# Operand splits behind accumulator hand-backs, earlier weight loads and a copy in two parts, in a hybrid attention and recurrence block

## The chip, the cores and the metric

The kernel runs as one program on one core of a Trainium2 chip. The core has a matrix engine (TensorE, "PE" in the profile, with its weight loads as "PEld"), a vector engine (VectorE, "DVE"), a scalar engine (ScalarE, "ACT"), GpSimd ("POOL"), SyncE ("SP", which here does nothing but issue transfers), and DMA engines that move data between HBM and the on-chip memory. TensorE's results go to PSUM, eight banks of 128 x 512 fp32; everything else that is on chip lies in SBUF.

The metric is the time of one execution on the device, in microseconds (us), lower being better. Times are medians of several executions.

## The reference

One encoder block over a sequence of 1024 tokens with 1024 channels, all in fp32. `@` is a matrix product.

```python
xn = rmsnorm(x, norm1_g)
q_sb, k_sb, v_sb, f_raw, i_hg, q_hg, g_hg, gate_sb, gate_hg = split(xn @ w_in)
# stick-breaking attention, 8 heads of 64, strictly causal (s < t)
z = q @ k.T / sqrt(64)
A[t, s] = sigmoid(z[t, s]) * prod_{s<j<t} (1 - sigmoid(z[t, j]))
o_sb = A @ v
# HGRN2 recurrence, 4 heads of 128, in chunks of 64 tokens
f = lb + (1 - lb) * sigmoid(f_raw)
S_t = diag(f_t) S_{t-1} + (1 - f_t) i_t^T ;  o_t = S_t^T silu(q_t)
o_hg = rmsnorm(o_hg) * silu(g_hg)
# merge by gates, output projection, MLP, final norm
merged = sigmoid(gate_sb + b) * (o_sb @ w_o_sb) + sigmoid(gate_hg + b) * (o_hg @ w_o_hg)
h = x + merged @ w_out
h = h + square(relu(rmsnorm(h, norm2_g) @ w_ff1)) @ w_ff2
return rmsnorm(h, final_g)
```

## The kernel before

**Products.** An fp32 matrix is kept as two parts of the reduced type `fp32r`, a high part (a cast of the value) and a low part (the value less its high part). `hi_lo` makes both: the cast is a copy on ACT (L144), the subtraction runs on DVE (L149) and waits for the cast. This is called a split below. A product of two split matrices is three matmuls for each step of the contraction (high by high, high by low, low by high), so a `128 x 512` result with 512 channels in the contraction takes twelve matmuls, issued by `three` at L121. The large products use Strassen-like forms: sums and differences of blocks stand as operands, and there are fewer products than blocks.

**Order of the work.** The Tile framework schedules the program: it keeps data dependences, gives each engine a queue that runs in order, and otherwise follows the order of the program. `after(ins, earlier)` adds an order on an engine without any wait in hardware. TensorE's work is in two lanes ("main" and "fill", L88 to L117), each in order. `load` (L129) issues a transfer from SP and ties each to the one before it, so that these leave SP in the order of the program; a load whose buffer is not yet free holds up every load behind it. In the output stage, `in_turn` (L136) also ties ACT's and DVE's instructions to the order of the program, among them all casts and subtractions of `hi_lo`.

**Buffers.** SBUF holds 40 slots of 128 x 1024 fp32 (`slot`), 10 halves of 128 x 512 (`half`), and the pool `wts` with two buffers for each of three tags: `raw` (weights as loaded), `whi` and `wlo` (their two parts). A new tile of a tag waits until the tile two before it has been read for the last time. `Unit` (L419) is a set of weights: `load` puts its pieces in `raw` buffers, or in slots for those pieces that its tuple `roomy` names; `split` loads what is not loaded, and makes the high and low parts (in slots where the unit is `wide`).

**Stages that the change touches**, in order of time:

- Attention. For each head and each block of 128 queries, `scores` makes the products with the keys, ACT takes two sigmoids into `bt` and `rm`, and `weights` (L768) runs a scan over the keys on DVE (L778), multiplies (`mul`, L157), and copies the result `bt` by a transfer from SP into `wr`, an `fp32r` tile. `turn` (L818) transposes `wr` on TensorE in parts of four key blocks, which ACT copies out of PSUM (`pw`), and `values` multiplies by the values (`po`). The last query block, number 7, has 1024 keys; its scan and product are made in two parts, columns 512 to 1022 first, then 0 to 511, and one copy of all 1024 columns follows. Its `turn` transposes columns 512 to 1023 first, then calls `between`, the value products of the head before, and then transposes columns 0 to 511.
- Gate products of the first kind. `raw_job(cb)`, for eight column blocks, loads and splits the weights `wga*` and makes three products. `st.prefetch()` inside splits the next job's weights and loads those of the job after it.
- Attention output. `sb_job(cp)`, four jobs, multiplies the attention output by `w_o_sb` (`wo00` to `wo03`, 512 KB each). Its unit is loaded by the prefetch, into `raw` buffers.
- Gate pairs. `gates` goes through eight `GatePair` objects. Each starts product 6 into bank `gX` (`x6`), whose result DVE adds into `gu` (L1201), then product 5 into bank `gY` (`y5`), then product 7 on top of `gX` (`x7`), a product with the HGRN2 output, and product 3 on top of `gY`. Between `y5` and `x7` the next pair's weights are split (`n.split`): two subtractions on raw weights (`wg*r`), a split of four blocks, one more subtraction and a second split. The casts and low parts are tied behind the DVE addition `gu` by `behind`; the first two subtractions are not.
- Output projection. `out_start` makes the Strassen forms of `merged @ w_out`. Each form has a weight operand (`wout*`, for the forms named `11`, `21`, `2`, `3`, `4`, `1` and `22`) and a merged operand (`m2`, `m3`, `ma`, `m1`, `m4`, two tiles each, read back from the scratch tensors `fd`). A form runs over four token blocks of twelve matmuls each. Forms `11` and `12` accumulate in four banks `pwW`, forms `2`, `3` and `a` in four banks `pwX`; after each token block DVE adds or subtracts the bank into the residual tiles `h` (L1204 for the subtractions), and with that it hands the bank back to TensorE, which starts the next form on the same bank. `out_operands` loads and splits the operands of a form two forms ahead, with its splits at the place where it is called. `out_block_done` makes forms `1` and `4` with banks `pwY`.
- First weights of the MLP. `UpPair.load`, `split` and `sums` bring the first `w_ff1` pairs and make sums of blocks of them in place, on DVE, four subtractions for each pair. The sums of the first two pairs stand in the fourth loop of `out_start`; the loop over `out_block_done` follows (L2228), then the MLP.

## Time and profile before

| | |
|---|---|
| median of 3 runs | 1426.67 us (1425.78 to 1429.88) |
| the profiled execution's own time | 1428.57 us |
| its span, first to last instruction | 1426.8 us |
| mean granted TensorE clock | 0.996 |
| ACT busy | 677.1 us (47%) |
| DMA, mean over the span | 172 GB/s |

The stretches that hold the stages named above, in a view of busy time by windows (length, then busy time and number of instructions of PE, PEld, DVE, ACT and POOL, then the granted clock, the share of the DMA engines' time that is busy, and GB/s):

```profile
0.00:120.00 120.00, 115.41 (x738) 101.55 (x740) 84.60 (x123) 80.81 (x172) 26.05 (x71) 1.00 0.58 166
120.00:500.00 380.00, 379.13 (x3677) 325.52 (x3674) 235.15 (x350) 188.16 (x444) 43.26 (x106) 1.00 0.41 110
500.00:590.00 90.00, 89.97 (x729) 74.80 (x728) 70.14 (x99) 42.50 (x87) 18.86 (x25) 1.00 0.71 209
590.00:725.00 135.00, 132.09 (x581) 108.63 (x580) 104.08 (x151) 44.77 (x61) 10.79 (x20) 1.00 0.55 181
725.00:800.00 75.00, 72.10 (x318) 59.11 (x317) 54.61 (x65) 36.69 (x48) 11.11 (x19) 0.98 0.73 231
800.00:1426.80 626.80, 619.61 (x2772) 513.34 (x2770) 448.16 (x536) 284.19 (x387) 30.01 (x43) 1.00 0.55 196
```

Attention and the recurrence take the first 500 us; the gate products of the first kind and the attention output end near 590, the gate pairs near 725, the output projection soon after 800, and the MLP takes the rest.

How to read the lines of the profile below. A line of a group or of one instruction has its start (for one instruction), its length or the group's busy time in us, the engine, the line of the code, the operation, then `out<-in` by the names of the tiles, the sizes as partitions x elements, and in square brackets the idle time just before it with what ended that wait. `SPq` is SyncE's queue, where a line is the issue of a transfer; a line with `DMA` is the flight of one, from its start to its landing. A line such as `PE gX L121 <- DVE gu L1201: 2.9, 2, 2.4` belongs to the list of waits: TensorE's work for tile `gX` waited for DVE's work on `gu`, 2.9 us in all, in two waits, the longest 2.4. In the list of stretches, "granted clock" is TensorE's clock as a share of full speed.

### The profile page before, as it was taken

The page shows a single profiled execution, that of the slowest core. Times are in us where ns is not written, and L with a number is a line of the kernel's source. Part 1 is how long each engine was busy: PE and PEld are TensorE (multiplying, and loading weights), DVE is VectorE, ACT ScalarE, POOL GpSimd, SP SyncE. Part 2 cuts the span into 40 slices and gives each one's busy share as a digit, 9 for nine tenths or more (in the row PEclk, how much of TensorE's full clock was granted, in tenths as well). Part 3 has the DMA queues.
Part 4 walks back from the last instruction along what each step waited for, and adds up shares of the span by engine and source line. Part 5 has one row for each costly group of instructions (what it writes and reads, how often), then busy time and mean ns, then how long its engine had stood idle before and what let it go on. Part 6 is the DMA issues. An engine that isn't in the chain of part 4 may idle for free.

```text
span 1426.8 us, 22645 instructions
## 1 busy us (share of the span) xinstructions
PE 1408.3 (99%) x8806; PEld 1182.9 (83%) x8806; DVE 996.7 (70%) x1320; ACT 677.1 (47%) x1197; POOL 140.1 (10%) x283
## 2 busy tenths in 40 slices
PE   9999999999999999999999999999999999999998
PEld 8888888988888888788887888888888888888886
DVE  6587677656635586788659897766666658668765
ACT  7576666643323354332244764454444443524343
POOL 3121121110000022000010300000000000000042
PEclk9999999999999999999999999999999999999999
DMA  7356366632203458744587515443346974776825
GB/s 215 97 169 185 104 170 150 154 79 81 74 24 111 112 173 242 235 156 159 182 243 249 181 39 186 162 151 135 140 157 235 342 268 155 273 276 235 285 95 182
DMA packets 167139, 244.78 MB, mean 172 GB/s; under 512 B 26700, under 2 KB 97912, under 8 KB 167032
## 3 DMA queue, kind: packets, MB, share of 16 engines
q1 hardware_dynamic: 151192, 200.07, 41.3%
q0 software_dynamic: 11520, 34.61, 9.9%
q10 hardware_dynamic: 4320, 8.65, 1.7%
q8 instruction: 69, 1.13, 0.3%
q14 instruction: 38, 0.31, 0.1%
HBM read 162.55 MB, written 61.87 MB: 157 GB/s over the span
## 4 chain that ended last, share of the span: by engine, by line
PE 85%; DMA 4%; DVE 2%; ACT 1%; issue 0%; POOL 0%; SPq 0%; DVEq 0%; POOLq 0%
PE pm L121 21%; PE pX L121 9%; PE pW L121 6%; PE pY L121 6%; PE pji L121 3%; PE pga L121 3%; PE pjf L121 3%; PE pjg L121 3%; PE pjq L121 3%; PE gX L121 3%; PE pyh L121 3%; PE gY L121 3%; PE pys L121 2%; PE po L121 2%; PE z L121 2%; PE pjqk L121 2%
## 5 line engine op out<-in xcount | busy, mean ns | idle before, releaser
L778 DVE TENSOR_TENSOR_SCAN rm<-rm,bits 128x511 f32<-128x511 f32 (+7 forms) x72 | 87.3, 1222 | 39.7 <-ACT rm L756 39.6
L144 ACT CAST whid<-w 128x1024 fp32r<-128x1024 f32 x30 | 31.6, 1053 | 154.6 <-PE pm L121 90.3
L121 PE MATMUL pm<-wlod,sh 128*128 128x512 f32 x240 | 93.5, 389 | 0.0
L121 PE MATMUL pm<-whid,sh 128*128 128x512 f32 x240 | 93.4, 389 | 0.0
L121 PE MATMUL pm<-whid,sl 128*128 128x512 f32 x240 | 93.4, 389 | 0.0
L121 PE MATMUL pm<-tl,sh 128*128 128x512 f32 (+1 forms) x210 | 81.3, 387 | 0.0
L121 PE MATMUL pm<-th,sl 128*128 128x512 f32 (+1 forms) x210 | 81.3, 387 | 0.0
L121 PE MATMUL pm<-th,sh 128*128 128x512 f32 (+1 forms) x210 | 81.3, 387 | 0.0
L149 DVE TENSOR_TENSOR wlod<-w,whid 128x1024 fp32r<-128x1024 f32 x30 | 36.7, 1222 | 59.2 <-ACT whid L144 59.2
L149 DVE TENSOR_TENSOR sl<-sa,sh 128x1024 fp32r<-128x1024 f32 x56 | 68.2, 1217 | 0.5 <-ACT sh L144 0.5
L144 ACT COPY wT<-pw 128x128 f32<-128x128 f32 (+3 forms) x96 | 43.9, 483 | 34.8 <-PE pw L818 29.9
L144 ACT CAST sh<-sa 128x1024 fp32r<-128x1024 f32 x56 | 57.2, 1046 | 6.0 <-DMA sa<-ad 6.0
L1955 POOL TENSOR_SCALAR fss<-fss 128x1 f32<-128x1 f32 x8 | 4.5, 562 | 562.1 <-ACT fsc L1950 561.6
L157 DVE TENSOR_TENSOR bt<-bt,rm 128x511 f32<-128x511 f32 (+7 forms) x72 | 48.9, 687 | 8.8 <-ACT bt L759 3.0
L121 PEld LDWEIGHTS pm<-wlod,sh 128*128 128x128 f32 x240 | 45.1, 188 | 9.9 <-DVE wlod L149 0.4
L121 PEld LDWEIGHTS pm<-whid,sh 128*128 128x128 f32 x240 | 45.0, 188 | 9.4
L121 PEld LDWEIGHTS pm<-whid,sl 128*128 128x128 f32 x240 | 45.0, 188 | 9.2
L756 ACT ACTIVATE rm<-z 128x511 f32<-128x511 f32 (+4 forms) x96 | 48.3, 505 | 4.4 <-DMA wr<-bt 2.3
L759 ACT ACTIVATE bt<-z 128x512 f32<-128x512 f32 (+3 forms) x96 | 48.6, 508 | 3.4 <-DMA wr<-bt 2.5
L121 PE MATMUL pX<-sql,t1h 128*128 128x512 f32 x128 | 50.0, 391 | 0.1
L121 PE MATMUL pX<-sqh,t1l 128*128 128x512 f32 x128 | 49.8, 389 | 0.0
L121 PE MATMUL pX<-sqh,t1h 128*128 128x512 f32 x128 | 49.8, 389 | 0.0
(913 smaller groups left out, 4334.6 us busy)
## 6 DMA issues: line engine op xcount, KB each, us to landing
w<-in_w_ff_dram SPq DMA_DIRECT2D x72, 512.0 KB, 5.0
sa<-ad SPq DMA_DIRECT2D x56, 512.0 KB, 6.8
ad<-a SPq DMA_DIRECT2D x32, 256.0 KB, 4.3
ad<-s SPq DMA_DIRECT2D x16, 512.0 KB, 5.4
tw<-in_w_out_dram POOLq DMA_DIRECT2D x24, 256.0 KB, 4.5
x<-in_x_dram SPq DMA_DIRECT2D x8, 512.0 KB, 8.5
wr<-bt SPq DMA_DIRECT2D x8, 512.0 KB, 3.1
xnl<-xnh POOLq DMA_DIRECT2D x8, 512.0 KB, 13.8
```

What stands on the lines that cost most here:

```text
L121: return pe(nc.tensor.matmul(*a, **k))
L144: hi_last[0] = after(in_turn("act", nc.scalar.copy(dst, src)), hi_behind[0])
L149: nc.vector.tensor_tensor(out=dst, in0=src, in1=hi.bitcast(F32), op=ALU.subtract),
L157: return nc.vector.tensor_tensor(out=out, in0=a, in1=b, op=ALU.mult)
L756: nc.scalar.activation(rm[:, s0 + c0 - 1 : s0 + m - 1], z[:, c0:m], AF.Sigmoid, scale=-0.125)
L759: nc.scalar.activation(bt[:, s0 : s0 + e], z[:, :e], AF.Sigmoid, scale=0.125)
L778: nc.vector.tensor_tensor_scan(out=rr, data0=rr, data1=bits[:, 1024 - nk + a : 1024 - nk + b][:, ::-1], initial=rm[:, b : b + 1] if i else ...
L1955: nc.gpsimd.tensor_scalar(out=ssq, in0=ssq, scalar1=1.0 / D, scalar2=EPS, op0=ALU.mult, op1=ALU.add)
```

## The change

The diff does the following.

- In `weights` the copy into `wr` moves into the loop over the two parts, so that each part is copied right after its product; the copy of the first part of query block 7 takes columns 512 to 1023 (with the last column, which GpSimd sets to zero). Blocks with one part still have one copy.
- In `raw_job`, in the seventh and eighth jobs, two `w_o_sb` units each are loaded right after the prefetch, and piece 0 of these units lies in a slot in place of a `raw` buffer. Before, the prefetch asked for one of them in each of these two jobs and for the others during the attention output.
- In `GatePair.split` the first subtraction is tied behind `gu` too.
- `out_operands` now takes one weight operand or one merged operand, loads it, and returns its split, which the caller runs later; the tiles for the high and low parts of a merged operand are taken at the split. The weight units `3` and `1` lie in slots, the others in `raw` buffers. In the loops of `out_start` each load comes as early as before or earlier, and each split stands behind the hand-back of a token block.
- The weight sums of the first two MLP pairs move from the last loop of `out_start` into the loop over `out_block_done`, behind the hand-backs of blocks 0 and 1, and the splits of those pairs move behind the hand-backs of their loop.

```diff
--- before.py
+++ after.py
@@ -773,6 +773,7 @@
         bt, rm = zs[h, qb]
         cut = qb == NT - 1
         parts = ((512, nk - 1), (0, 512)) if cut else ((0, nk - 1),)
+        wr = slot_n(f"wr{h}_{qb}", nk, F32R)
         for i, (a, b) in enumerate(parts):
             rr = rm[:, a:b][:, ::-1]
             nc.vector.tensor_tensor_scan(
@@ -784,8 +785,8 @@
                 op1=ALU.max,
             )
             weighted[0] = mul(bt[:, a:b], bt[:, a:b], rm[:, a:b])
-        wr = slot_n(f"wr{h}_{qb}", nk, F32R)
-        nc.sync.dma_start(wr[:, 0:nk].bitcast(F32), bt[:, 0:nk])
+            cs = slice(a, nk if i == 0 else b)
+            nc.sync.dma_start(wr[:, cs].bitcast(F32), bt[:, cs])
         zs[h, qb] = wr
 
     def turn(h, qb, between):
@@ -1297,6 +1298,9 @@
                 u.split_t()
             st.prefetch()
             hi_behind[0] = None
+            if cb >= KT - 2:
+                for unit in sb_units[2 * (cb - KT + 2) : 2 * (cb - KT + 3)]:
+                    unit.load()
             yield from steps_of(p4, 1, 0, 1, 4, True)
             add(p14, p1, p4)
             if cb == 3 or cb == KT - 1:
@@ -1367,9 +1371,13 @@
         yield from range(4)
         gp[0].split()
 
+    sb_units = []
+
     def sb_job(cp):
         src = W_OSB[:, cp * 256 : (cp + 1) * 256].rearrange("(k p) c -> p k c", p=P)
         unit = Unit(f"wo0{cp}", [[(0, 256, src)]])
+        unit.roomy = (0,)
+        sb_units.append(unit)
 
         def body():
             if cp == 0:
@@ -1439,7 +1447,7 @@
             cb = self.cb
             r0, r1 = self.raw
             s0, s1 = slice(0, 512), slice(512, 1024)
-            sub(r0[:, s0], r0[:, s1], r0[:, s0])
+            after(sub(r0[:, s0], r0[:, s1], r0[:, s0]), behind)
             sub(r1[:, s0], r1[:, s1], r0[:, s0])
             h, l = (
                 wpool.tile([P, 1024], F32R, tag=t, name=f"{t}g{cb}") for t in ("whi", "wlo")
@@ -1601,28 +1609,29 @@
     out_form = {"11": out_unit("11", out_block(0, 0))}
     merged = {}
 
-    def out_operands(w=(), m=(), behind=False):
-
-        for n in w:
-            out_form[n] = out_unit(n, tw[int(n)] if len(n) == 1 else out_block(int(n[0]) - 1, int(n[1]) - 1))
-            out_form[n].split()
-        for n in m:
-            merged[n] = []
-            raw = []
-            for kp in range(2):
-                r = slot(f"m{n}r{kp}")
-                load(r.rearrange("p (k t) -> p k t", k=2), fd[n][kp])
-                h, l = slot(f"m{n}h{kp}", F32R), slot(f"m{n}l{kp}", F32R)
-                merged[n].append((h, l))
-                raw.append(r)
-
-            def split(n=n, raw=raw):
-                for (h, l), r in zip(merged[n], raw):
-                    hi_lo(h, l, r)
-
-            if behind:
-                return split
-            split()
+    def out_operands(w=None, m=None):
+
+        if w:
+            unit = out_form[w] = out_unit(
+                w, tw[int(w)] if len(w) == 1 else out_block(int(w[0]) - 1, int(w[1]) - 1)
+            )
+            unit.roomy = (0, 1) if w in ("3", "1") else ()
+            unit.load()
+            return unit.split
+        merged[m] = []
+        raw = []
+        for kp in range(2):
+            r = slot(f"m{m}r{kp}")
+            load(r.rearrange("p (k t) -> p k t", k=2), fd[m][kp])
+            raw.append(r)
+
+        def split():
+            for kp, r in enumerate(raw):
+                h, l = slot(f"m{m}h{kp}", F32R), slot(f"m{m}l{kp}", F32R)
+                merged[m].append((h, l))
+                hi_lo(h, l, r)
+
+        return split
 
     def out_product(ps, a, w, tb, start):
         open_block("fill")
@@ -1652,7 +1661,8 @@
             nc.scalar.dma_start(hres[4 + tb], X[rows(4 + tb), :])
         for tb in range(4):
             if tb == 0:
-                out_operands(["21"])
+                out_operands("21")()
+                w2 = out_operands("2")
             oW[tb] = bank(f"pwW{tb}")
             out_product(oW[tb], "11", "11", tb, True)
             for ins in (
@@ -1662,19 +1672,20 @@
                 in_turn("act", ins)
             h = hres[4 + tb][:, right]
             turn_dve(sub(h, h, oW[tb]))
-            if tb == 0:
-                out_operands(["2"])
             if tb == 1:
-                m2 = out_operands(m=["2"], behind=True)
+                m2 = out_operands(m="2")
+                w2()
         m2()
         for tb in range(4):
+            if tb == 0:
+                w3 = out_operands("3")
+            if tb == 1:
+                m3 = out_operands(m="3")
             out_product(oW[tb], "12", "21", tb, False)
             h = hres[4 + tb][:, left]
             turn_dve(add(h, h, oW[tb]))
-            if tb == 0:
-                out_operands(["3"])
-            if tb == 1:
-                out_operands(m=["3"])
+            if tb == 2:
+                w3()
         for tb in range(4):
             oX[tb] = bank(f"pwX{tb}")
             out_product(oX[tb], "2", "2", tb, True)
@@ -1682,30 +1693,42 @@
             turn_dve(sub(h, h, oX[tb]))
             nc.gpsimd.dma_start(hres[tb], X[rows(tb), :], accum_op=ALU.add)
             if tb == 0:
-                out_operands(["4"])
+                m3()
+                w4 = out_operands("4")
             if tb == 1:
-                out_operands(m=["a"])
+                ma = out_operands(m="a")
+            if tb == 3:
+                w4()
         for tb in range(4):
             out_product(oX[tb], "3", "3", tb, False)
             h = hres[tb][:, right]
             turn_dve(sub(h, h, oX[tb]))
             if tb == 0:
-                out_operands(["1"])
+                ma()
+                w1 = out_operands("1")
             if tb == 1:
-                out_operands(m=["1"])
+                m1 = out_operands(m="1")
             if tb > 1:
                 pairs[tb - 2].load()
+            if tb == 3:
+                w1()
 
         for tb in range(4):
             u = pairs[tb % 2]
-            (u.split if tb < 2 else u.sums)()
             out_product(oX[tb], "a", "4", tb, False)
             h = hres[tb][:, left]
             turn_dve(add(h, h, oX[tb]))
+            if tb == 0:
+                m1()
+                w22 = out_operands("22")
+            if tb == 1:
+                m4 = out_operands(m="4")
+            if tb < 2:
+                u.split()
             if tb == 2:
-                out_operands(["22"])
+                w22()
             if tb == 3:
-                out_operands(m=["4"])
+                m4()
 
     def out_block_done(tb):
 
@@ -2227,6 +2250,8 @@
 
     for tb in range(NT):
         out_block_done(tb)
+        if tb < 2:
+            first[tb].sums()
         norm_from(tb)
         if tb > 0:
             norm_to(tb - 1)
```

## The prediction

> **What bounds the kernel now.** First the page, then the list of what TensorE waited for, then busy time and clock in the stretches around its longest waits.
>
> ```profile
> span 1426.8 us, 22645 instructions
> PE 1408.3 (99%) x8806; PEld 1182.9 (83%) x8806; DVE 996.7 (70%) x1320; ACT 677.1 (47%) x1197; POOL 140.1 (10%) x283
> PE pw L818 <- DMA wr<-bt: 2.9, 3, 1.8
> PE gX L121 <- DVE gu L1201: 2.9, 2, 2.4
> PE pwX L121 <- DVE h L1204: 2.9, 2, 2.1
> 115.59:119.00 3.41, 1.65 (x12) 1.05 (x10) 2.69 (x3) 3.37 (x9) 1.08 (x3) 1.00 0.89 249
> 119.00:122.41 3.41, 3.41 (x20) 2.25 (x21) 3.28 (x6) 1.75 (x3) 0.52 (x1) 0.50 0.57 185
> 590.04:593.45 3.41, 2.17 (x10) 1.47 (x8) 1.96 (x4) 0.00 (x0) 0.37 (x1) 1.00 1.00 343
> 593.45:596.86 3.41, 2.22 (x10) 1.84 (x11) 1.46 (x3) 2.84 (x4) 0.17 (x1) 1.00 0.67 268
> 757.30:760.71 3.41, 1.35 (x7) 1.06 (x7) 3.16 (x4) 2.68 (x4) 0.00 (x0) 1.00 0.55 180
> 760.71:764.12 3.41, 3.41 (x10) 2.67 (x9) 3.41 (x5) 1.40 (x2) 0.00 (x0) 0.50 0.97 307
> ```
>
> TensorE is busy 1408.3 of 1426.8 us. The change removes none of its matmuls, so all it can win is idle time (18.5 us) and time at a lowered clock. The list shows three waits of 2.9 us each that belong to the places the diff touches. In the window rows the columns are the stretch, its length, busy time of PE, PEld, DVE, ACT, POOL, then granted clock, DMA share and GB/s. Where TensorE was busy 1.65 or 1.35 us of a 3.41 us stretch, the stretch after it was granted 0.50; where 2.43 us of waiting straddled two stretches (busy 2.17 and 2.22), the clock stayed at 1.00. So two of the three waits cost a second time: 3.41 us at half clock lose 3.41 x 0.5 = 1.71 us of work each.
>
> **Part A, the longest copy in two.** For query block 7 the weights are made in two column parts, and one copy of 1024 columns waits for both.
>
> ```profile
> 110.32 0.69 DVE L157 TENSOR_TENSOR bt<-bt,rm 128x511 f32<-128x511 f32 x1 [0.19 <-issue]
> 113.24 5.16 DMA wr<-bt
> 118.53 0.50 PE L818 MATMUL pw<-ident_r,wr 128*128 128x128 f32 x4 [1.76 <-DMA wr<-bt]
> 58.86 0.51 PE L818 MATMUL pw<-ident_r,wr 128*128 128x128 f32 x4 [0.30 <-DMA wr<-bt]
> 209.33 0.34 PE L818 MATMUL pw<-ident_r,wr 128*128 128x128 f32 x2 [0.87 <-DMA wr<-bt]
> 202.08 7.11 DMA wr<-bt
> 155.47 4.05 PE po L121 x40
> ```
>
> The first four transposes of this block read columns 512 to 1023, exactly the part that DVE had multiplied by 111.01 (110.32 + 0.69). The copy started at 113.24, after the second part, and landed 5.16 us later. Split, the first half can start at about 111.1, 2.1 us sooner. With as long a flight it lands at 116.3; TensorE wants it at 118.53 - 1.76 = 116.8. The second half still lands near 118.4, but is read only after the value products between (40 instructions, 4.05 us at full clock), about 121. So 1.76 goes, with its slow window (1.71), and the 0.30 at 58.86 as well. The wait at 209.33 is for a block with one copy, 7.11 us on its way, and stays. Added: eight DMA issues on SP, below 0.5 us each, while SP stands idle most of the time; queued behind them are weight loads, which would wait for the mul, at most 2 us. I cost them at nothing, and at 0.87 (the worst wait left here) if loads bunch. The gain is the earlier start; what the smaller size saves in flight I leave out. **A: 1.76 + 0.30 + 1.71 = 3.77 us.**
>
> **Part B, gate splits behind hand-backs.**
>
> ```profile
> 591.49 0.69 DVE L1204 TENSOR_TENSOR wg4r<-wg4r 128x512 f32<-128x512 f32 x1 [3.43 <-DMA wg4r<-in_w_in_dram]
> 593.90 0.68 DVE L1201 TENSOR_TENSOR gu<-pr,gX 128x512 f32<-128x512 f32 x1
> 594.64 0.50 PE L121 MATMUL gX<-gsh,tgh 128*128 128x512 f32 x1 [2.43 <-DVE gu L1201]
> 694.40 0.68 DVE L1201 TENSOR_TENSOR pr<-pr,gY 128x512 f32<-128x512 f32 x1
> 698.18 0.39 PE L121 MATMUL gY<-gsh,whig 128*128 128x512 f32 x1
> 600.37 2.77 PE gY L121 x12
> ```
>
> `gu` reads the bank that TensorE wants back. DVE is in order, and the next pair's first subtraction stood ahead of `gu`, waiting 3.43 us for its weights. Tied behind `gu`, it lets `gu` run when product 6 ends, one product of twelve matmuls (2.7 us) before TensorE asks at 592.2: 2.43 us gone. What waits now is the split: three subtractions (0.69 + 1.28, two of them in the second row) move from before `gu` to after it, in each of seven pairs. Their products are a whole pair later, so TensorE does not see them; the nearest reader behind them on DVE is `pr<-pr,gY`, which frees a bank 698.18 - 695.08 = 3.1 us before it is wanted. Moved subtractions (1.97) plus one exposed ACT cast (1.05, as for `wout3h` below) make 3.0: just covered, and DVE may take `gY` first. Bounds: 0 to 7 pairs x 0.5 us; I take 0, by that row. The other wait on `gu` (2.9 - 2.4 = 0.5) comes in the last pair, which has no next one to split: it stays. The attention-output weights now come in slots, so the two raw buffers of the gate weights fall free sooner; that makes `wg4r` early and helps B a second time, at no gain of its own. **B: 2.43 us.**
>
> **Part C, output-projection splits behind hand-backs.**
>
> ```profile
> 747.24 1.05 ACT L144 CAST wout3h<-wout3r 128x1024 fp32r<-128x1024 f32 x1 [0.90 <-DMA wout3r<-tw]
> 749.75 1.05 ACT L144 CAST m3h<-m3r 128x1024 fp32r<-128x1024 f32 x1 [0.16 <-DMA m3r<-fd]
> 740.24 1.22 DVE L149 TENSOR_TENSOR m2l<-m2r,m2h 128x1024 fp32r<-128x1024 f32 x1 [5.10 <-ACT m2h L144]
> 748.33 1.22 DVE L149 TENSOR_TENSOR wout3l<-wout3r,wout3h 128x1024 fp32r<-128x1024 f32 x1 [0.72 <-ACT wout3h L144]
> 750.07 2.35 DVE L149 TENSOR_TENSOR m3l<-m3r,m3h 128x1024 fp32r<-128x1024 f32 x2
> 753.53 0.68 DVE L1204 TENSOR_TENSOR h<-h,pwX 128x512 f32<-128x512 f32 x1
> 758.69 0.68 DVE L1204 TENSOR_TENSOR h<-h,pwX 128x512 f32<-128x512 f32 x1
> 754.36 0.47 PE L121 MATMUL pwX<-wout3h,m3h 128*128 128x512 f32 x1 [0.84 <-DVE h L1204]
> 759.43 0.50 PE L121 MATMUL pwX<-wout3h,m3h 128*128 128x512 f32 x1 [2.06 <-DVE h L1204]
> 731.69 1.96 SPq L129 DMA_DIRECT2D m3r<-fd  x2
> 747.63 2.32 SPq L129 DMA_DIRECT2D wout4r<-tw  x2
> ```
>
> Both waits are hand-backs (`h<-h,pwX`) queued on DVE behind splits of late weights; the second stood behind `wout4`, whose load left SP only at 747.63. I lay DVE out in the new order from these rows. `wout3` lands as before; its split ends at 749.5. Then the fourth add of form 12 (0.6), the first hand-back of form 2 (to 750.7), `m3` (2 x 1.2, cast done at 750.8, to 753.1), and three hand-backs (to 754.9). TensorE ends form 2 at 754.36 - 0.84 = 753.5 and needs bank 0 (750.7) and both `m3` tiles (the second after six matmuls, 754.9): no wait; block 1, at 756.2, has its bank since 753.7. `wout4r` is no longer held to 747.63 by the raw buffers, since `wout3r` is in slots: it can be issued behind `m3r`, about 734, and lands in order behind it, near 753; its split ends near 757, needed at 764. The later sets (`ma`, `1`, `m1`, `22`, `m4`) lie the same way, with 4 us or more. So 0.84 + 2.06 goes, and the window at half clock. If the splits slip by more than the 0.4 us between `m3` and form 3, part of it stays: bounds 0 to 4.6, value 4.6 by the rows. **C: 2.90 + 1.71 = 4.61 us.**
>
> **Part D, loads asked sooner, and weight sums.**
>
> ```profile
> 514.47 1.57 SPq L129 DMA_DIRECT2D wga7r<-in_w_in_dram  x2
> 523.39 1.22 DVE L1204 TENSOR_TENSOR wga7r<-wga7r,wga7r 128x1024 f32<-128x1024 f32 x1 [4.45 <-DMA wga7r<-in_w_in_dram]
> 533.66 0.37 SPq L129 DMA_DIRECT2D wo02r<-in_w_o_sb_dram  x1
> 550.57 1.05 ACT L144 CAST wo02h<-wo02r 128x1024 fp32r<-128x1024 f32 x1 [7.22 <-DMA wo02r<-in_w_o_sb_dram]
> 788.62 1.28 DVE L1589 SCALAR_TENSOR_TENSOR hn<-h,n_y,g2b 128x1024 f32<-128x1024 f32 x1 [1.61 <-POOL n_y L243]
> ```
>
> Asked near 517, the 2 MB of attention-output weights miss the crowd in which `wo02r` took 17 us. TensorE lost nothing there, so nothing is won. Cost: they follow `wga7r`, on which DVE waits 4.45 us; in order behind it they take nothing, sharing with it up to 9 us (17 less the 7.6 from 515.7 to 523.3). I take 0: the transfers above landed in the order asked. The eight sums (0.69 each by the `wg4r` row, 5.5 us) leave a full DVE for one that stands idle 1.61 us before `hn`; the first hand-back there comes sooner by more. 0.
>
> **Sum.** The profiled execution took 1428.57 us, 1.77 beside its span. 1428.57 - (3.77 + 2.43 + 4.61) = 1428.57 - 10.81 = **1417.8 us**. The median of the runs shown, 1426.67, is 1.9 lower; their spread, 1425.78 to 1429.88, is what one or two slow windows make. A run without stalls has none to lose, so I keep 1417.8; if the 1.9 belongs to the profiling, it is 1415.9.
>
> [...]
>
> **Rivals.**
> 1. Operands late. Form 3 finds `m3` instead of the bank: the 0.4 us of C is too thin, and its waits and dip return as operand waits. 1417.8 + 4.6 = 1422.4. For it: `wout3r` took 16 us. Against: bank and operands come 0.4 us early or more by the rows.
> 2. The first half of the copy flies longer beside new traffic: A is lost, 1421.6. For: one copy took 7.11 us before 209.33. Against: 5.16 suffices.
> 3. The dips come from something other than these waits and stay: 1421.2. Against: both follow them at once.
> 4. The change does not do what it says: the order on the engines comes out as before, or equal waits take the place of the old ones: 1428.6.
> 5. Slower: in the output stage eight transfers of 512 KB (`wout4`, `ma`, `wout1`, `m1`) now stand beside `m2`, `wout3` and `m3`. At 307 GB/s they take 13.7 us. If the queue shares its rate instead of finishing in order, `m3` lands up to that much later: 11 us of waiting, 1.7 of slow clock, and some 4 more for `m2`, whose split ends at 741.46, 1.2 us before its use (four blocks of 2.7 before 753.5): 1417.8 + 16.7 = 1434.5. It decides from a delay of 13 us in all. Against it: the casts of `wout3` and `m3` were released one after another, 1.2 to 2 us apart, which is order.
>
> **How the numbers follow.** Forecast 0.60 (1415.5 to 1420), rivals 0.12, 0.06, 0.05, 0.08, 0.09. A measurement of this kernel tells 0.3% (4.3 us) from nothing: faster is below 1422.4. Forecast, 2, 3 and half of 1 give 0.77; half of 1 and rival 4 give 0.14; rival 5 gives 0.09. From 1414.5 (1415.9 less the waits that I leave in) to 1423.5 some 0.83 lie.
>
> **What would show it.** The list of TensorE's waits without `wr<-bt` at the first two places, without `gu` near 590 and without `h` near 755; `gu` ahead of `wg4r` on DVE; `wout4r` issued before 740; a granted clock of 1.00 from 20 to 1400 us. Wrong: a wait of `pwX` on `m3` or `wout3`, of `gY` on `pr`, of `pga` on `wga7wlo` above 0.5, or a window at 0.50 with none of these before it.

## The result, and the profile after

The changed kernel took 1417.88 us (median of 6 runs, 1416.70 to 1418.38), the kernel before 1427.09 us (6 runs, 1422.42 to 1432.32): a ratio of 0.9931, with a 95% interval of 0.9909 to 0.9953. The forecast was 1417.8. The total was right; two of the three terms that made it were too large, and the loads, which were costed at nothing, were worth more when put in alone than either of these two was when undone. The experiments below show this.

The page of the kernel after, its first lines:

```profile
span 1415.9 us, 22663 instructions
PE 1403.9 (99%) x8806; PEld 1180.7 (83%) x8806; DVE 997.4 (70%) x1320; ACT 678.3 (48%) x1197; POOL 143.4 (10%) x283
```

The list of what TensorE waited for, in the kernel after (total, times, longest):

```profile
PE warm L121 <- POOL ident masks.py:199: 2.2, 1, 2.2
PE hnt L124 <- DVE hn L1597: 1.0, 1, 1.0
PE pX L121 <- DVE a L1202: 0.6, 1, 0.6
PE pX L121 <- DVE sql L149: 0.3, 1, 0.3
PE pjqk L121 <- DVE xnl L325: 0.3, 1, 0.3
```

The span of the profiled execution is 10.9 us shorter, with the same 8806 matmuls. TensorE's idle time fell from 18.5 to 12.0 us, and its busy time by 4.4 us, of which two slow stretches (2 x 1.71) make 3.4. None of the three groups of 2.9 us is left, nor the smaller waits in them that the forecast had left in (0.87 at 209 us, 0.5 in the last gate pair). A wait of `hnt` for `hn`, 1.0 us, is new.

Busy time and clock in the stretches that answer to those before (PE, PEld, DVE, ACT, POOL, then granted clock, DMA share, GB/s):

```profile
114.84:118.26 3.42, 3.42 (x28) 2.60 (x28) 2.50 (x2) 3.33 (x8) 0.50 (x2) 1.00 1.11 286
...
745.83:749.25 3.42, 3.42 (x17) 2.83 (x16) 3.42 (x4) 2.83 (x3) 0.00 (x0) 1.00 1.04 389
```

Form 3 began at 744.88 here, 9.5 us sooner than before, so the second row lies sooner too. TensorE is full and the clock is whole at both places. The timeline of the kernel after, around the first gate pair and in the output projection (start, length, engine, instruction):

```profile
584.60 0.69 DVE L1202 TENSOR_TENSOR gu<-pr,gX 128x512 f32<-128x512 f32 x1 [3.38 <-PE gX L121]
585.21 0.68 DVE L1205 TENSOR_TENSOR wg4r<-wg4r 128x512 f32<-128x512 f32 x1
...
725.89 2.05 SPq L129 DMA_DIRECT2D wout4r<-tw  x2
...
734.00 0.39 PE L121 MATMUL pwX<-wout2h,m2h 128*128 128x512 f32 x1
...
735.56 2.14 ACT L144 CAST wout3h<-wout3r 128x1024 fp32r<-128x1024 f32 x2 [5.01 <-DMA wout3r<-tw]
737.99 1.05 ACT L144 CAST m3h<-m3r 128x1024 fp32r<-128x1024 f32 x1 [0.29 <-DMA m3r<-fd]
739.28 1.05 ACT L144 CAST m3h<-m3r 128x1024 fp32r<-128x1024 f32 x1 [0.24 <-DMA m3r<-fd]
```

The order is the one forecast: `gu` runs when product 6 ends and the weights' subtraction follows it; `wout4r` is asked for at 725.89, before 740; and the operands of form 3 land one after another, about 1.3 us apart, though `wout4` had been asked for behind them. So the slower rival, in which these transfers share their rate, did not come about.

### The profile page after: what moved, and what is told of

Same layout as the page of the kernel before. It is cut to its first block, busy times and chain, and to the rows that moved or that the text cites. A ratio compares the mean times of both kernels' runs of the same rounds, so it can differ in the third digit from the quotient of the medians.

```text
span 1415.9 us, 22663 instructions
## 1 busy us (share of the span) xinstructions
PE 1403.9 (99%) x8806; PEld 1180.7 (83%) x8806; DVE 997.4 (70%) x1320; ACT 678.3 (48%) x1197; POOL 143.4 (10%) x283
## 4 chain that ended last, share of the span: by engine, by line
PE 92%; DVE 2%; DMA 2%; ACT 1%; issue 1%; POOL 1%; SPq 0%; DVEq 0%; POOLq 0%; ACTq 0%
PE pm L121 21%; PE pX L121 9%; PE pY L121 6%; PE pjqk L121 5%; PE pW L121 5%; PE pji L121 3%; PE pjv L121 3%; PE pga L121 3%; PE pjf L121 3%; PE pjg L121 3%; PE pjq L121 3%; PE pys L121 3%; PE pyh L121 3%; PE gY L121 3%; PE gX L121 3%; PE z L121 3%
```

## The experiments

The changed kernel was run twice, 1417.88 and 1417.12; an undone part is set against both, since not all runs were on one chip. Only two of the undone kernels, "loads back" and "no tie and loads back", ran beside the changed kernel on one chip, so for the others a difference of about 1 us may belong to the chip.

The kernel before, which ran beside every set, spreads more than any of these: 87 executions in all lie between 1419.23 and 1432.50 with a median of 1425.1, and two sets on one chip had medians of 1423.00 and 1426.20. The ratios in the table move with that, so parts are compared by their times. Against 1425.1 the whole change gains 7.2 to 8.0 us, against the six executions beside it 9.2.

| kernel | median, us | range (runs) | ratio to before, 95% |
|---|---|---|---|
| changed kernel | 1417.88 | 1416.70 to 1418.38 (6) | 0.9931 (0.9909 to 0.9953) |
| changed kernel again | 1417.12 | 1416.68 to 1417.81 (4) | 0.9925 (0.9910 to 0.9940) |
| kernel before again | 1424.32 | 1420.77 to 1429.09 (10) | 0.9986 (0.9967 to 1.0005) |
| one copy | 1418.85 | 1418.47 to 1420.05 (6) | 0.9956 (0.9942 to 0.9970) |
| no tie | 1418.55 | 1417.65 to 1419.95 (6) | 0.9959 (0.9941 to 0.9977) |
| loads back | 1418.31 | 1416.63 to 1420.11 (4) | 0.9937 (0.9921 to 0.9954) |
| no tie and loads back | 1422.26 | 1420.47 to 1425.19 (7) | 0.9968 (0.9955 to 0.9980) |
| output stage as before | 1419.82 | 1417.35 to 1420.69 (7) | 0.9957 (0.9940 to 0.9974) |
| splits at their loads | 1417.60 | 1416.88 to 1419.84 (10) | 0.9957 (0.9941 to 0.9973) |
| sums back | 1419.97 | 1418.05 to 1422.17 (10) | 0.9955 (0.9939 to 0.9971) |
| sums later | 1417.15 | 1416.22 to 1417.96 (7) | 0.9950 (0.9931 to 0.9970) |
| before, loads alone | 1420.29 | 1417.48 to 1426.16 (12) | 0.9964 (0.9949 to 0.9979) |
| longer `gu` | 1455.16 | 1454.89 to 1455.42 (2) | 1.0217 (1.0181 to 1.0253) |

### Part A undone: one copy

```diff
-            cs = slice(a, nk if i == 0 else b)
-            nc.sync.dma_start(wr[:, cs].bitcast(F32), bt[:, cs])
...
+        nc.sync.dma_start(wr[:, 0:nk].bitcast(F32), bt[:, 0:nk])
```

> The changed kernel with one copy of 1024 columns for query block 7, as before. Theory (part A is worth its two waits and a slow window): TensorE waits for wr<-bt near 58 us (0.3) and near 116 us (1.8) come back, and the stretch after the second is granted 0.50, so 1417.9 + 0.3 + 1.8 + 1.7 = 1421.7. Rival 1 (the slow window has another cause): the two waits come back but the clock stays at 1.00, 1420.0. Rival 2 (the split copy was not what removed the wait): no wait above 0.3, 1417.9. Open beside it: the wait of 0.87 at 209 us, in a block with one copy, which the forecast left in and which is gone from the changed kernel. If it comes back here, the split copy removed it too, and the time is 0.9 higher.

The wait of 0.30 near 58 us came back, the wait of 1.76 did not, and no slow stretch. The time rose by 1.0 to 1.7 us, of which the list of waits shows the 0.30; where the rest lies is open. The timeline of this kernel has the same copy and its transposes:

```profile
113.60 1.11 SPq L788 DMA_DIRECT2D wr<-bt  x2
...
116.98 0.46 PE L818 MATMUL pw<-ident_r,wr 128*128 128x128 f32 x4
```

The copy left at 113.60, where it left at 113.24 in the profile before; the transposes started without waiting at 116.98, so it was on its way for less than 3.4 us, not 5.16. So in this kernel the wait is gone without the split copy; the next section shows that in the kernel before it recurs. The wait near 205 to 209 us (0.87 before, gone in the first profile after) was 0.7 here; it comes and goes between executions of one kernel, as the next profiles show.

### The kernels unedited, once more

> The changed kernel again, unedited, as the measure for the others on this chip. Theory (its stalls do not depend on the execution, but for waits for copies): 1417.9 within 0.7, a wait of hnt for hn of 1.0, granted clock 1.00 from 20 to 1400 us, and a wait of pw for wr<-bt near 205 us that may be anything from 0 to 1.5. Rival (the one execution with that wait at 0 was the typical one): no wait for wr<-bt.

> The kernel before again, unedited. Theory (its waits for copies change from one execution to the next, with the flight of the copies, and its waits for DVE do not): gX for gu 2.4 and pwX for h 2.9 are there again, within 0.5, pw for wr<-bt is anything from 0.3 to 3, and a slow stretch stands behind each wait that leaves TensorE idle for more than about 1.7 us of one stretch of 3.41. Rival (all its waits recur): pw for wr<-bt is 2.9 again, with the 1.76 near 118 us.

The changed kernel again showed `hnt` for `hn` 1.0 and `pw` for `wr<-bt` 0.7, at a whole clock. The kernel before (10 runs, 1420.77 to 1429.09) showed in part other waits than in its first profile. Its list of TensorE's waits:

```profile
PE gX L121 <- DVE gu L1201: 3.8, 2, 3.5
PE warm L121 <- POOL ident masks.py:199: 2.2, 1, 2.2
PE pkv L121 <- ACT pp L1109: 1.9, 1, 1.9
PE pwX L121 <- DVE h L1204: 1.7, 1, 1.7
PE pw L818 <- ACT bt L759: 1.7, 1, 1.7
```

The last line is the wait of Part A under another name. In the timeline:

```profile
113.18 1.11 SPq L788 DMA_DIRECT2D wr<-bt  x2
...
118.42 0.51 PE L818 MATMUL pw<-ident_r,wr 128*128 128x128 f32 x4 [1.70 <-ACT bt L759]
```

These are the same four transposes, which waited 1.76 in the first profile. ACT's `bt` ended at 118.28, so the list names it, but with one copy in the changed kernel the same transposes ran at 116.98, before ACT came to that `bt` (118.06). What they waited for is the copy. Its landing is recorded in sixteen parts: fifteen had come by 116.20 in the first profile and by 116.11 here, and the last one came at 118.40 and 118.28, flights of 5.16 and 5.10 us. In the kernel with one copy all sixteen came by 116.66, 3.06 us after the issue, and in the kernel with the sooner loads alone (below) by 116.27, 3.05 us after it. So the wait belongs to the kernel before and not to one execution; no slow stretch followed it this time (TensorE was busy 1.91 us in the stretch from 114.81). A transfer of instructions of 16 KB began at 114.17 and 114.30 in the two profiles with the late part, while the copy was on its way, and at 120.0 and 119.4 in the two without. No run moves that transfer by itself, so whether it makes the part late is not shown.

ACT and TensorE in its timeline, later on:

```profile
540.08 1.05 ACT L144 CAST wo01h<-wo01r 128x1024 fp32r<-128x1024 f32 x1 [10.56 <-DMA wo01r<-in_w_o_sb_dram]
...
542.30 0.97 ACT L1109 COPY pp<-pk 128x512 f32<-128x512 f32 x2 [0.45 <-ACT g L1306]
...
542.93 0.49 PE L121 MATMUL pkv<-v,pp 128*128 128x128 f32 x2 [1.93 <-ACT pp L1109]
```

So the rival was right on the longest wait for a copy, while the smaller one near 209 us fell from 0.87 to 0.2, as the theory had it. For the rest the expectation failed: `gu` rose from 2.4 to 3.5, `pwX` fell from 2.9 to 1.7, and a wait of 1.93 appeared where TensorE had lost nothing. There ACT stood 10.56 us before the cast of `wo01`, with the copies for `pkv` queued behind it. Each of these three waits goes back to the landing of a load, and the landing moves.

### Part B and the sooner loads, one by one and together

```diff
-            after(sub(r0[:, s0], r0[:, s1], r0[:, s0]), behind)
+            sub(r0[:, s0], r0[:, s1], r0[:, s0])
```

> The changed kernel without the tie of the first weight subtraction behind gu, so that three subtractions of the next pair stand ahead of gu on DVE, as before. Theory (the tie is what removed the wait of 2.43): gX waits for gu again, 1417.9 + 2.4 = 1420.3. Rival (the sooner loads removed it, and the tie does nothing more): the raw weights of the fifth pair have landed by 584.7 us, the subtractions end near 586.1 and gu near 586.7, before TensorE asks for the bank at 587.1, so no wait above 0.2 and 1417.9.

```diff
-            if cb >= KT - 2:
-                for unit in sb_units[2 * (cb - KT + 2) : 2 * (cb - KT + 3)]:
-                    unit.load()
...
-        unit.roomy = (0,)
```

> The changed kernel with the attention-output weights asked for as before, in raw buffers; the tie behind gu stays. Theory (either of tie and sooner loads removes the wait of gX for gu): the raw weights of the fifth pair land near 591 us again, behind gu, and no wait of gX above 0.5; the time is that of the changed kernel on this chip, within 0.5. Rival (the sooner loads alone do it, and the tie gains nothing): a wait of 1 to 2.4 for gu comes back, or the split that now stands behind gu makes gY or the next pair wait by as much.

> The changed kernel with neither the tie nor the sooner loads. Theory (either one is enough): the wait of gX for gu comes back, 2.4, and the time is 2.4 above that of the changed kernel on this chip. Rival (that wait of before was of one execution only, as that at 118 us was): below 0.5.

Without the tie, from the timeline:

```profile
585.15 0.69 DVE L1205 TENSOR_TENSOR wg4r<-wg4r 128x512 f32<-128x512 f32 x1 [1.96 <-DMA wg4r<-in_w_in_dram]
586.54 1.29 DVE L1205 TENSOR_TENSOR wg4r<-wg4r,wg4r 128x512 f32<-128x512 f32 x2 [0.69 <-DMA wg4r<-in_w_in_dram]
587.75 0.68 DVE L1202 TENSOR_TENSOR gu<-pr,gX 128x512 f32<-128x512 f32 x1
588.88 0.19 PEld L121 LDWEIGHTS gX<-gsh,tgh 128*128 128x128 f32 x1
```

`gu` stands behind the three subtractions, as before, and still ends at 588.43, ahead of TensorE at 588.88: the rival held, and the tie is not needed at this place. Its list has one wait of `gX` for `gu`, 0.3, in the last pair. With the loads back and the tie kept, no wait of `gX` either: the theory held there. With both undone the time rose by 4.4 to 5.1 us, though each alone cost 0.4 to 1.4. The profile of that kernel, from a run at the lower end of its range (1420.98), shows 1.1 of `gX` for `gu` in two waits, the longest 0.8, so what made the slower runs is not seen. Its runs spread over 4.7 us, those of the changed kernel over 1.7.

### The sooner loads alone

The kernel before, with the lines of the diff above put in.

> The kernel before with one edit of the change: the attention-output weights asked for in the seventh and eighth gate jobs, into slots. Theory (these loads, which the forecast costed at nothing, carry about half of the gain, since they free the raw buffers for the gate pairs and let ACT's casts of wo01 and wo02 run at once): no wait of pkv for pp, gX waits for gu below 0.5, and the time is 3 to 4.5 below that of the kernel before in the same rounds, a ratio near 0.9975. Rival 1 (the forecast: they are worth nothing by themselves): a ratio of 1.000 within 0.001. Rival 2 (they need the other parts; sharing the queues with the last gate weights, they cost what they gain): 1.000 to 1.003, with a wait of pga for wga7wlo of 0.5 or more.

What TensorE waited for in it, without the start:

```profile
PE pwX L121 <- DVE h L1204: 1.3, 2, 0.8
PE hnt L124 <- DVE hn L1596: 0.7, 1, 0.7
...
PE gX L121 <- DVE gu L1201: 0.3, 1, 0.3
```

A ratio of 0.9964 (0.9949 to 0.9979), 5.1 us of 1426, with an interval from 3.0 to 7.3: somewhat more than the theory said. The list has no wait of `pkv`, and that of `gu` is down to 0.3. The first profile of the kernel before had no wait of `pkv` either, so its absence in one profile says little; the wait for `gu` was 2.9 and 3.8 in both. The list also lacks the wait of 1.7 near 118 us, though this edit stands far behind it and the copy is whole; that much of the 5.1 is not due to what these loads do for the gates. With 3.4 us left, the part that the forecast costed at nothing still brings a third or more of the gain by itself.

### Part C: the output stage as before, and only its splits as before

In the first kernel `out_operands` and the loops of `out_start` are those of before, with the weight sums where the change put them. In the second the loads stay where the change put them, and each split stands at its load:

```diff
             turn_dve(add(h, h, oW[tb]))
-            if tb == 2:
+            if tb == 0:
                 w3()
+            if tb == 1:
+                m3()
...
-                m3()
-                w4 = out_operands("4")
+                out_operands("4")()
```

> The changed kernel with the loads and splits of the output projection as before (the weight sums stay in the loop over the row blocks). Theory: pwX waits for h twice, 0.8 and 2.1, and the stretch after the second is granted 0.50: 1417.9 + 2.9 + 1.7 = 1422.5. Rival 1 (the slow window has another cause): 1420.8. Rival 2 (the waits of before came from transfers made late elsewhere, not from the place of the splits): below 1418.5. Open beside it: the wait of gX for gu in the last pair (0.48 before, none after) comes back here if the loads of the output stage removed it.

> The changed kernel with the loads of the output projection where the change put them, but each split where its load is asked for (behind that block's hand-back), as the kernel before had it. Theory (the place of the splits on DVE is what counts): pwX or pwW waits for h, 1 to 3 us, as with the whole part undone, 1.9 above the changed kernel or more. Rival (the sooner loads alone do it): no wait of pwX or pwW for h above 0.3, and the time of the changed kernel.

The first list has TensorE's longest wait for DVE with the whole stage undone, the second with the splits alone undone:

```profile
PE pwX L121 <- DVE h L1205: 1.3, 2, 1.2
```

```profile
PE pwX L121 <- DVE h L1205: 0.8, 1, 0.8
```

With the stage undone the time rose by 1.9 to 2.7 us between the medians (1.5 to 1.9 between the means), not 4.6; the wait came back at 1.2, without a slow stretch, in a run of 1417.77. Its seven runs lie in two groups, three from 1417.35 to 1417.98 and four from 1419.82 to 1420.69. With only the splits undone, seven of ten runs lie at 1416.88 to 1418.18, the level of the changed kernel, and three at 1419.26 to 1419.84; the profile is of one of these. That the sooner loads do most of it, and the place of the splits keeps the rest from happening in some executions, is likely and not shown: three of seven against seven of ten are few, and on two chips. A slow stretch would fit the distance of the groups, 2 us, but the one profile of an upper group shows none, so what makes these groups stays open.

### The weight sums

```diff
+            if tb > 1:
+                u.sums()
             out_product(oX[tb], "a", "4", tb, False)
...
-        if tb < 2:
-            first[tb].sums()
```

> The changed kernel with the weight sums of the first two pairs back in the last loop of the output start, ahead of the products of blocks 2 and 3. Theory (the new wait of hnt for hn, 1.0 us, comes from the sums: the POOL instruction on n_ss took 3.59 us while six of them ran on DVE back to back, and 0.19 in the kernel before): n_ss takes below 0.5 us at its first block, the wait is gone, 1417.9 - 1.0 = 1416.9. Rival 1 (POOL's length has another cause, such as the first use of its code): n_ss stays above 3 us and the wait stays, 1417.9. Rival 2 (the sums push the hand-backs of the last loop): pwY or pwX waits for h by 0.5 to 2 us, 1417.9 to 1419.

```diff
-        if tb < 2:
-            first[tb].sums()
...
+        if tb in (2, 3):
+            first[tb - 2].sums()
```

> The changed kernel with the weight sums of the first two pairs two blocks later, behind the norm of blocks 0 and 1. Theory (the wait of hnt for hn has two sides: with the sums in the last loop DVE reaches the first hand-back of the row blocks late, and with the sums behind it they hold up POOL's n_ss): n_ss takes below 0.5 us at its first block, hn of block 1 ends near 778, ahead of the transposes at 780.3, the wait of 1.0 is gone, and the time is 1.0 below that of the changed kernel (1417.1 to 1417.9 in its two sets): 1416.1 to 1416.9. Rival (the sums now push the hand-backs of blocks 4 and 5 or the norms of blocks 2 and 3): a wait of pwY for h or of hnt for hn of 0.5 to 1.5 takes its place, 1417 to 1418.

The new wait in the timeline of the changed kernel:

```profile
773.32 0.68 DVE L1205 TENSOR_TENSOR w_0r<-w_0r,w_0r 128x512 f32<-128x512 f32 x1
...
773.48 3.59 POOL L239 TENSOR_SCALAR n_ss<-n_ss 128x1 f32<-128x1 f32 x1 [47.91 <-ACT hn L1587]
...
776.33 0.68 DVE L1205 TENSOR_TENSOR w_1r<-w_1r,w_1r 128x512 f32<-128x512 f32 x1
...
777.75 1.29 DVE L1597 SCALAR_TENSOR_TENSOR hn<-h,n_y,g2b 128x1024 f32<-128x1024 f32 x1 [0.74 <-POOL n_y L243]
```

with the sums back:

```profile
778.51 0.19 POOL L239 TENSOR_SCALAR n_ss<-n_ss 128x1 f32<-128x1 f32 x1 [52.73 <-ACT hn L1587]
...
779.39 1.28 DVE L1597 SCALAR_TENSOR_TENSOR hn<-h,n_y,g2b 128x1024 f32<-128x1024 f32 x1 [1.55 <-POOL n_y L243]
...
782.74 0.44 PE L124 MATMUL hnt<-ident,hn 128*128 128x128 f32 x2 [1.68 <-DVE hn L1597]
```

and with the sums later:

```profile
775.09 0.19 POOL L239 TENSOR_SCALAR n_ss<-n_ss 128x1 f32<-128x1 f32 x1 [47.91 <-ACT hn L1587]
...
776.28 1.28 DVE L1597 SCALAR_TENSOR_TENSOR hn<-h,n_y,g2b 128x1024 f32<-128x1024 f32 x1 [0.47 <-POOL n_y L243]
```

Both sides are seen. Behind the hand-backs, POOL's `n_ss` took 3.59 us, with six sums in a row on DVE beside it, against 0.19 in the other two kernels. The transposes that wait are those of the next block, whose `n_ss` follows on POOL. Ahead of the hand-backs, `n_ss` took 0.19, but DVE is full until 777.8 and the first norm starts at 779.39, so the wait grows to 1.68: the theory's step was right and its result wrong. The time grew by 2.1 to 2.9 us, of which the longer wait is 0.7; the rest is not explained. Two blocks later the norm starts at 776.28 and the wait of 1.0 is gone (0.4 is left in a later block). That kernel took 1417.15 us, which can't be told from the changed kernel's 1417.12 and 1417.88; its profile also caught a wait of 0.8 of `pga` for `wga7wlo`, the last gate weights of the first kind, which its edit does not reach. That is the sign that the forecast had named against the sooner loads; it stands in one of the ten profiles that have these loads.

### What makes a slow stretch

The addition `gu` is repeated in seven gate pairs, with the same sum again:

```diff
+    TIMES = {0: 0, 4: 5, 1: 7, 5: 6, 2: 8, 6: 7, 3: 6, 7: 5}
...
-            self.u2_sum = add(self.u2, self.p[:, 0:512], self.X)
+            for _ in range(1 + TIMES[self.cb]):
+                self.u2_sum = add(self.u2, self.p[:, 0:512], self.X)
```

> The changed kernel with the addition gu repeated 5 to 8 times more in seven of the gate pairs (the same sum again), so that TensorE stands idle before its product 7 for about 0.60 us a repeat less the 1.75 that gu has to spare: near 1.25, 1.85, 2.45 and 3.05 us, 14 us in all. Theory (a stretch of 3.41 us is granted 0.50 when TensorE was idle for more than about half of the stretch before it, and the stretches follow one another without regard to the work): a slow stretch behind each wait that leaves more than 1.7 us of one stretch idle, none behind those that two stretches share, three or four in all, 1417.5 + 14 + 6 = 1437. Rival 1 (a whole stretch must be idle): none, 1431.5. Rival 2 (any wait over 1.7 us brings one): five, 1440.

1455.16 us. The seven waits were 1.7 to 5.3 us long, 23.8 in all, since a repeat cost 0.82 us and not 0.60 ((23.8 + 7 x 1.75) / 44 repeats, with other work of DVE between some of them); hence more time and more slow stretches than the 1437 us and the three or four expected. Nine stretches were granted 0.50, six of them full (1.71 lost in each) and three with 1.44, 0.49 and 2.27 busy (half of that lost): 12.3 us, and 1417.5 + 23.8 + 12.3 = 1453.6, 1.6 below the measured time. Some of them, in the view by windows (length, PE busy, granted clock, DMA share, GB/s):

```profile
603.05:606.46 3.41, 1.21 (x5) 1.00 0.00 0
606.46:609.87 3.41, 3.41 (x9) 0.50 0.00 0
...
691.79:695.20 3.41, 0.90 (x4) 1.00 0.00 0
695.20:698.61 3.41, 2.27 (x5) 0.50 0.02 5
698.61:702.03 3.42, 3.42 (x9) 0.50 0.05 7
...
736.17:739.58 3.41, 1.69 (x7) 1.00 0.88 293
739.58:742.99 3.41, 3.41 (x16) 1.00 0.58 168
```

A stretch with 1.21 busy was followed by a slow one, a stretch with 1.69 was not; the profile before has one with 1.65 that was, and its two slow stretches, from 119.00 and 760.71, begin 641.71 us apart, 188 times 3.4133. Both rivals fall: the first asked for a whole idle stretch, and the second for any wait over 1.7, which the last one (1.72) was, as was the 2.43 of the profile before, which straddled two stretches.

## Why the prediction was right, and where not

- **The total.** It was worked out from the profiled execution's own time, by taking away every stall that the change reaches. It came out because the change does leave few stalls in any execution: the waits of the changed kernel without the start are 2.2 us, and its runs lie within 1.7 us where those of before lie within 9.9. By the medians of one comparison the gain is 9.2 us, and 7.2 to 8.0 against all executions of the kernel before, where 10.81 was forecast from an execution 1.9 above the median then shown. That the sum came within 0.1 us is luck in part: by the parts as measured below, A and C were forecast 4.0 to 5.5 us too large, B and D 2.0 to 2.7 too small, and the execution that the sum started from was 3.5 us above the median of 1425.1, which takes up what is left.
- **Part A** failed in size. The step "So 1.76 goes, with its slow window (1.71)" was right on the wait of the kernel before, which came in both profiles (1.76 and 1.70); its slow stretch came in one of them, where TensorE was busy 1.65 us in the stretch of the wait, and not in the other, where it was busy 1.91. But the flight of 5.16 us hung on one late part of sixteen, and in the changed kernel that part is not late: with one copy there is no wait, so the split copy wins little there. Undone, the part costs 1.0 to 1.7 us, not 3.77.
- **Part B** named the wrong cause, or one of two. "Tied behind `gu` ... 2.43 us gone" holds only while the weights are late; the loads of part D, which the forecast saw to "help B a second time, at no gain of its own", remove the wait by themselves. The split moved behind `gu` cost nothing, as forecast.
- **Part D** is the step that failed most. "TensorE lost nothing there, so nothing is won" was true of the one profile, in which ACT stood 7.22 us before the cast of `wo02`. The same queueing cost TensorE 1.93 us in the next profile, and late loads feed the wait for `gu` (2.43 and 3.51 us in the two profiles). B and D together are worth 4.4 to 5.1 us, D alone 5.1, or 3.4 without the wait near 118 us. Its other half, the sums, was costed at nothing and brought the wait of 1.0, with a POOL instruction of 3.59 us in place of 0.19; the profile before had a milder case at the same place, the second `n_ss` with 1.18 us beside the `hn` of 788.62, and the forecast did not use it.
- **Part C** had the mechanism right (hand-backs queued behind splits of late weights) and the size wrong: 1.9 to 2.7 us, not 4.61. The 2.06 us that made a slow stretch was one execution's; others had 1.2 and 1.7, without one.
- **The sum of the parts** as measured, A 1.0 to 1.7, B with D 4.4 to 5.1, C 1.9 to 2.7, is 7.3 to 9.5 us, against 9.2 between the medians, or 7.2 to 8.0. No large rest is seen, but each part is uncertain by about 1 us, so the agreement is rough.
- **The rivals.** Operands late: `m3`'s second cast began at 739.28, its split ended on DVE at 742.46, and TensorE came to form 3 at 744.88, 2.4 us later, more room than the 0.4 us of the forecast. The dips stay: both went with their waits, and with idle time put into the gate pairs nine stretches were granted 0.50. The slower rival: the operands of form 3 landed one after another, about 1.3 us apart.

## What to carry to other kernels

A wait in one profile that ends with the landing of a transfer can be a sample and not a constant: before pricing it, take a second profile, since some of these waits recurred at the same place (1.76 and 1.70 here, under two names) and others moved (that of `pkv`, none and 1.93). Look also whether an engine queue upstream (here ACT before a cast, DVE before a subtraction) stands idle for many us on the same kind of transfer, since that is where the next execution may lose its time. A load asked for earlier can be worth more than the order of the work that waits for it, even where TensorE loses nothing in the profile at hand. A wait can also go by an edit that does not touch it, as that near 118 us did, so a kernel's time alone does not say which part won it. And where the edits remove one wait by two means, undo them one by one and together: here each alone was worth 0.4 to 1.4 us and both together 4.4 to 5.1.

## What the runs showed of the hardware

- **The clock.** Of the stretches of 3.41 us at a whole clock, those with 1.65 and 1.35 us of TensorE's work in the profile before, with 1.27 in the second profile of that kernel, and with 1.21 and 0.90 with the longer `gu` were each followed by one granted 0.50. Those with 2.17 and 2.22 in the profile before, with 1.91 in the second, and with 1.69 with the longer `gu` were followed by one granted 1.00. With the longer `gu`, a stretch at 0.50 with 2.27 busy was followed by another at 0.50, and each of the six full ones by one at 1.00. In the profile before, the wait of 2.06 us cost 1.71 us more in the stretch after it, and the wait of 2.43 us, which lay across two stretches, cost nothing more.
- **POOL beside DVE.** In the row blocks the first `n_ss`, an instruction of 128 x 1 on POOL, took 0.19 us with the sums back, where DVE stood idle beside it, and 0.19 with the sums later, at 775.09, beside subtractions that began at 774.50 and 775.11. In the changed kernel it took 3.59 us beside six subtractions on DVE that followed one another without a gap, and ended at 777.07, the last of them at 777.01.
- **Transfers.** Fifteen of the sixteen parts of the same 512 KB copy had landed 2.9 to 3.1 us after its issue in four profiles. The last part came with them in two kernels, and 2.2 us later in both profiles of the kernel before (5.16 and 5.10 us in all), in which a transfer of instructions of 16 KB began 0.93 and 1.12 us after the copy left; that the one makes the other is not shown.
